# Residual loads placed behind the output weights in the queue that issues them

## The chip, the cores and the metric

The kernel runs on one core of a Trainium2 chip. The metric is the time of one execution in device microseconds (us), as the median of several runs. Besides the runs there is one profiled execution; its trace is what the prediction reads. Engines are named as the profile names them: PE (TensorE: matmuls), PEld (its weight loads), DVE (VectorE), ACT (ScalarE), POOL (GpSimd) and SP (SyncE, which here only issues DMA transfers; SPq is its queue of issues).

## The reference

One layer of an encoder on `x` (1024 tokens x 1024 columns, float32). Three sub-layers follow each other, each with a norm before it and a norm on its output, which is then added to the residual stream. The change lies at the end of the first:

```python
mix = jnp.concatenate([attn_o, dn_o], axis=-1) @ w_out[l]
x = x + _rms_norm(mix, g_mix_post[l])
c = _memory_cross_attention(_rms_norm(x, g_cross_pre[l]), _rms_norm(mem, g_mem[l]),
                            w_cq[l], w_ckv[l], w_co[l])
x = x + _rms_norm(c, g_cross_post[l])
f = _swiglu(_rms_norm(x, g_ffn_pre[l]), w_gate_up[l], w_down[l])
x = x + _rms_norm(f, g_ffn_post[l])
```

`attn_o` comes from windowed attention, `dn_o` from a gated delta rule in chunks. `w_out` is 1024 x 1024. The old `x` is the residual that is added to the normed `mix`.

## The kernel before, in words

All operands of matmuls are split into a high and a low part (`split`, L101 to L106: ACT casts to the high part at L103, DVE or POOL subtracts it from the original to get the low part at L104), and each product is the sum of three matmuls: high x high, low x high, high x low.

**Order.** The kernel is written for Tile, whose scheduler fixes the order of instructions on every engine when the program is compiled. It simulates time: at each point an engine takes, of the instructions that are ready, the one with the highest priority. Priority is the order in which the code traces them; `tc.high_priority(AHEAD)` moves what a block traces 300 places forward. `tc.issue_after(ins)` adds an edge of order alone: what the block traces on the engine of `ins` is queued behind `ins` on that engine, without a wait for its end. On the chip each queue then runs in the order so fixed, and a wait at its head holds all behind it.

**Weights.** `load_w` (L118 to L129) issues one 512 KB load of weights on SP (L125) into a tile `wraw`, and splits it into `whi` (ACT) and `wlo` (DVE or POOL). Each of the three tags has 2 buffers (`wp`, L116), so the third load waits until the first has been split. Both the load and the split are traced with high priority.

**The output projection.** Before it, L1147 loads `mix` (stored by the attention and the delta rule in `d_mix`) in two halves of 512 tokens: 4 loads of 512 KB each, into `mraw` for the first half and into a tile that the profile calls `b` for the second; each piece is split on ACT and DVE into `s0h`, `s0l` and into two `b` tiles. The last steps of the attention windows (`psw`, L685: scores; L687: mask and maximum on DVE; `ptw`, L712: transposes; `pow`, L717: values) are still under way at that time.

`mid_gemm` (L1087 to L1130) is called for the first half of the tokens (L1152) and then for the second (L1154). In each call:

- For each of 2 column halves it loads 4 pieces of `w_out` (256 rows x 512 columns, L1099), 8 in all, and runs 24 matmuls `pmg` with each (L1105). Then ACT squares the result and sums it (L1108), and DVE multiplies it with the gain into `z` (L1109).
- For each of 4 tiles of 128 tokens it loads 512 KB of residual rows, `xr`, on SP (L1115; tag `xr` has 4 buffers), gets the inverse root on POOL (L1117, L1118), and DVE adds the residual: z = z * rs + xr (L1119). `z` is stored (L1120). `xr` is then reused as the normed input of the cross-attention (L1122 to L1128).
- The second call runs `turn_norm` (L1071: transposes `ptn` on PE) on the first call's `xr` between its column halves.

The residual loads stand behind the eight weight loads in the code, but they depend on nothing else than a free buffer. After the two calls come loads of `d_mk` and `d_mv` (L1162) for the cross-attention and its query projection with weights `w_cq`.

Of the kernel before, what the change touches and what calls it, by code (L numbers as in the profile page):

```python
# [19 lines left out]
P = 128  # L20
# [56 lines left out]
def tile_hybrid_block(  # L77
# [6 lines left out]
    nc = tc.nc  # L84
# [15 lines left out]
    def split(hi, lo, src, scale=None, eng=None):  # L100

        if scale is None:
            nc.scalar.copy(hi, src)  # L103
            return (eng or nc.vector).tensor_tensor(lo, src, f32(hi), ALU.subtract)  # L104
        nc.scalar.activation(hi, src, AF.Identity, scale=scale)
        return nc.vector.scalar_tensor_tensor(lo, src, scale, f32(hi), ALU.mult, ALU.subtract)  # L106

    def pool(name, bufs, **kw):
        return tc.tile_pool(name=name, bufs=bufs, reuse_waits="tile", **kw)
# [5 lines left out]
    dram = ctx.enter_context(tc.tile_pool(name="dram", bufs=1, space=DRAM))  # L115
    wp = ctx.enter_context(pool("wp", 2))  # L116

    def load_w(src, k, n, eng=None, after=None, place=None):  # L118

        with tc.high_priority(AHEAD):  # L120
            raw = place or wp.tile([P, k, n], F32, tag="wraw", name="wraw")
            with ExitStack() as order_:
                if after:
                    order_.enter_context(tc.issue_after(after.ins))
                nc.sync.dma_start(raw, src.rearrange("(k p) n -> p k n", p=P))  # L125
            hi = wp.tile([P, k, n], F32R, tag="whi", name="whi")
            lo = wp.tile([P, k, n], F32R, tag="wlo", name="wlo")
            split(hi, lo, raw, eng=eng)
        return hi, lo  # L129
# [30 lines left out]
    def rstd_of(rs, ss, n, eps):  # L160

        w = ss.shape[-1]
        nc.gpsimd.tensor_scalar(rs, ss, n, eps, ALU.mult, ALU.add)
        nc.gpsimd.tensor_tensor(rs, rs, mhalf[:, :w], ALU.pow)
# [114 lines left out]
    def proj(src_cols, eng=None):  # L279
        whi, wlo = load_w(src_cols, KT, P, eng)  # L280
        pp = [pg.tile([P, 512], F32, tag="pg", name="pg") for _ in range(2)]
        gemm_b(whi, wlo, hT, pp)
        return pp
# [26 lines left out]
    for h in range(2):  # L310
        with tc.issue_after(ready[h][0].ins), tc.issue_after(ready[h][1].ins):
            ws.append(load_w(dcols(1, h), KT, P, after=xload[3]))
# [663 lines left out]
    def next_keys():  # L976

        ct = kv_done[0]
        kv_done[0] += 1
        whi, wlo = load_w(w_ckv[:, ct * P:(ct + 1) * P], KT, P, nc.gpsimd)  # L980
        pp = pc.tile([P, 512], F32, tag="pc", name="pck")[:, 0:ML]
        for k in range(KT):
            for i, (w, a) in enumerate(((whi, 0), (whi, 1), (wlo, 0))):
                nc.tensor.matmul(pp, w[:, k, :], mT[a][:, k, :], start=(k == 0 and i == 0), stop=(k == KT - 1 and i == 2))  # L984
        cv = mk.tile([P, 512], F32, tag="cv", name="cv", bufs=2)[:, 0:ML]
        nc.scalar.copy(cv, pp)
        nc.sync.dma_start(d_mk[ct * P:(ct + 1) * P, :], cv)
# [99 lines left out]
    def mid_gemm(tz, act, w, gp, res, dst, hf, between=None, banks=([PG] * 4, [PG] * 4), vec=False):  # L1087


        zs = [tz.tile([P, D], F32, tag="z", name="z", bufs=4) for _ in range(4)]  # L1090
        sss = [tz.tile([P, 2], F32, tag="zss", name="zss", bufs=8) for _ in range(4)]
        for ch in range(2):
            cs = slice(ch * 512, (ch + 1) * 512)
            if ch and between:
                between()

            pp = [q_.tile([P, 512], F32, tag=t_, name="pmg") for q_, t_ in banks[ch]]
            for kp in range(4):
                whi, wlo = load_w(w[kp * 256:(kp + 1) * 256, cs], 2, 512)  # L1099
                for t in range(4):  # L1100
                    tt = slice(t * P, (t + 1) * P)
                    for kk in range(2):
                        k = 2 * kp + kk
                        for i, (w_, a) in enumerate(((whi, 0), (whi, 1), (wlo, 0))):
                            nc.tensor.matmul(pp[t], act[a][:, k, tt], w_[:, kk, :], start=(k == 0 and i == 0),  # L1105
                                             stop=(k == KT - 1 and i == 2))
            for t in range(4):
                nc.scalar.activation(zs[t][:, cs], pp[t], AF.Square, accum_out=sss[t][:, ch:ch + 1])  # L1108
                nc.vector.tensor_tensor(zs[t][:, cs], pp[t], gp[:, cs], ALU.mult)  # L1109
        xn = []  # L1110
        for t in range(4):
            tok = slice(hf * HALF + t * P, hf * HALF + (t + 1) * P)
            z = zs[t]
            xr = tz.tile([P, D], F32, tag="xr", name="xr", bufs=XR)
            nc.sync.dma_start(xr, res[tok, :])  # L1115
            rs = tz.tile([P, 1], F32, tag="prs", name="prs", bufs=4)
            nc.gpsimd.tensor_scalar(rs, sss[t][:, 1:2], sss[t][:, 0:1], D * EPS, ALU.add, ALU.add)  # L1117
            nc.gpsimd.tensor_tensor(rs, rs, mhalf[:, 0:1], ALU.pow)  # L1118
            nc.vector.scalar_tensor_tensor(z, z, rs, xr, ALU.mult, ALU.add)  # L1119
            nc.sync.dma_start(dst[tok, :], z)  # L1120
            s2 = tz.tile([P, 1], F32, tag="ps2", name="ps2", bufs=4)
            nc.scalar.activation(xr, z, AF.Square, accum_out=s2)  # L1122
            r2 = tz.tile([P, 1], F32, tag="pr2", name="pr2", bufs=4)
            rstd_of(r2, s2, 1.0 / D, EPS)
            if vec:
                nc.vector.tensor_scalar(xr, z, r2, None, ALU.mult)
            else:
                nc.scalar.activation(xr, z, AF.Identity, scale=r2)  # L1128
            xn.append(xr)
        return xn  # L1130
# [12 lines left out]
    for hf in range(2):  # L1143
        for kp in range(4):
            k2 = slice(2 * kp, 2 * kp + 2)
            raw = raws[hf]
            nc.sync.dma_start(raw[:, k2, :], d_mix[kp * 256:(kp + 1) * 256, hf * HALF:(hf + 1) * HALF]  # L1147
                              .rearrange("(k p) t -> p k t", p=P))
            with tc.issue_after(marks[14].ins):
                split(mxT[hf][0][:, k2, :], mxT[hf][1][:, k2, :], raw[:, k2, :])  # L1150
    LR.close()
    xn0 = mid_gemm(tz, mxT[0], w_out, gp, x, d_x1, 0, banks=([PG] * 4, [PX] * 2 + [PN] * 2), vec=True)  # L1152
    h2T = [[opB.tile([P, KT, HALF], F32R, tag=b1, name=b1), opB_first[2]]]
    xn1 = mid_gemm(tz, mxT[1], w_out, gp, x, d_x1, 1, banks=([PG] * 4, [PX] * 2 + [PG] * 2),  # L1154
                   between=lambda: turn_norm(xn0, "cross", *h2T[0], pin=True))
    h2T.append(operand(opA, "s0"))
# [13 lines left out]
    raw = LR2.enter_context(pool("raw2", 1, side="right")).tile([P, KT, HALF], F32, name="oraw")  # L1170
# [239 lines left out]
    res = {}  # L1410
# [349 lines left out]
    def residual(t, after=None):  # L1760
        xr = tp_.tile([P, D], F32, tag="xrf", name="xrf")
        with tc.issue_after((after or late).ins):
            nc.sync.dma_start(xr, d_x2[there(t), :])
        return xr
# [62 lines left out]
    for t in range(4):  # L1827
# [19 lines left out]
        xr = residual(r)  # L1847
# [47 lines left out]
```

## Time and profile before

| | us |
|---|---|
| Median of 3 runs | 1499.31 (1497.92 to 1499.64) |
| The profiled execution | 1504.28 |
| Its span (first to last recorded work) | 1502.6 |
| PE busy in the span | 1469.4 (98%) |
| DVE busy | 1109.3 (74%) |
| ACT busy | 776.2 (52%) |

A row of the timeline gives start, duration (or, for several issues merged, the time from the first to the end of the last), engine, line, operation, out<-in and the count; in brackets stands how long the engine idled before it and what ended that. A row of a table by stretches gives from:to, its length, then busy time and count of the engines named, the granted clock of PE (1.00 is full), the busy share of the 16 DMA engines and GB/s. A row of waits names who waited for whom, the total, the number of times and the longest. All times count from the start of the span.

### The profile page before, as it was taken

How to read it: one execution, taken by the hardware profiler on the slowest of the kernel's cores; microseconds unless marked ns; L12 is line 12 of the kernel's file. 1: busy time of each engine (PE TensorE's matmuls, PEld its weight loads, DVE VectorE, ACT ScalarE, POOL GpSimd, SP SyncE). 2: the span in 40 equal slices, each digit the busy share in tenths (PEclk: the TensorE clock that was granted, in tenths of full speed). 3: DMA queues.
4: the chain of work that ended last, by engine and by line, in shares of the span. 5: the costliest groups of instructions: out<-in, count | busy, mean ns of one | idle time of the engine just before them, and what ended most of it. 6: DMA issues, size and time to landing. Idle time of an engine off the chain costs nothing.

```text
span 1502.6 us, 21339 instructions
## 1 busy us (share of the span) xinstructions
PE 1469.4 (98%) x7437; PEld 1239.6 (82%) x7437; DVE 1109.3 (74%) x1805; ACT 776.2 (52%) x1600; POOL 372.6 (25%) x410
## 2 busy tenths in 40 slices
PE   7999999999999999999999999999999999999998
PEld 6888877888889878888888877888888888888787
DVE  5878998577997866528767887676867764696666
ACT  7678844568467664555654774323223232444533
POOL 0011231442246203242201002343433342000030
PEclk9999999999999999999999999999999999999999
DMA  6244554656996585444855553443533433953355
GB/s 204 71 118 135 138 174 121 174 152 207 317 322 209 155 314 196 153 156 149 275 181 202 182 197 112 127 133 112 165 118 117 140 106 105 350 182 99 105 180 170
DMA packets 254168, 256.35 MB, mean 171 GB/s; under 512 B 18128, under 2 KB 186221, under 8 KB 254061
## 3 DMA queue, kind: packets, MB, share of 16 engines
q1 hardware_dynamic: 252141, 250.80, 52.7%
q0 software_dynamic: 768, 2.10, 0.5%
q10 hardware_dynamic: 1152, 2.10, 0.4%
q8 instruction: 58, 0.95, 0.3%
q14 instruction: 49, 0.40, 0.1%
HBM read 178.63 MB, written 73.70 MB: 168 GB/s over the span
## 4 chain that ended last, share of the span: by engine, by line
PE 68%; DVE 10%; DMA 4%; ACT 4%; issue 3%; SPq 1%; POOL 0%; DVEq 0%; ACTq 0%; POOLq 0%
PE pE L1511 7%; PE pD L1511 7%; PE pmg L1105 6%; PE pcq L276 6%; PE pdX L1733 6%; PE pA L1511 5%; PE pst L1324 5%; PE pB L1511 3%; PE pg L276 3%; PE psc L844 3%; PE pdA L1733 2%; PE pdD L1733 2%; PE pcs L1195 2%; PE pco L1222 1%; PE pck L984 1%
## 5 line engine op out<-in xcount | busy, mean ns | idle before, releaser
L103 ACT CAST whi<-wraw 128x1024 fp32r<-128x1024 f32 x96 | 100.6, 1049 | 123.3 <-DMA wraw<-in_w_gate_up_dram 39.5
L276 PE MATMUL pg<-hlo,whi 128*128 128x512 f32 x352 | 141.0, 401 | 0.0
L276 PE MATMUL pg<-hhi,whi 128*128 128x512 f32 x352 | 140.5, 399 | 0.0
L276 PE MATMUL pg<-hhi,wlo 128*128 128x512 f32 x352 | 140.2, 398 | 0.0
L104 POOL TENSOR_TENSOR wlo<-wraw,whi 128x1024 fp32r<-128x1024 f32 x36 | 88.0, 2444 | 175.8 <-ACT whi L103 163.7
L1511 PE MATMUL pA<-b,whi 128*128 128x512 f32 x352 | 109.8, 393 | 1.9 <-ACT whi L103 1.0
L104 DVE TENSOR_TENSOR wlo<-wraw,whi 128x1024 fp32r<-128x1024 f32 x60 | 74.1, 1235 | 36.1 <-ACT whi L103 31.8
L1511 PEld LDWEIGHTS pA<-b,whi 128*128 128x128 f32 x352 | 65.2, 188 | 17.1 <-ACT whi L103 1.9
L276 PEld LDWEIGHTS pg<-hhi,whi 128*128 128x128 f32 x352 | 67.3, 191 | 13.6 <-ACT hhi L241 0.3
L276 PEld LDWEIGHTS pg<-hhi,wlo 128*128 128x128 f32 x352 | 67.2, 191 | 12.6
L276 PEld LDWEIGHTS pg<-hlo,whi 128*128 128x128 f32 x352 | 67.0, 190 | 12.7
L1733 PE MATMUL pdX<-dhl,whi 128*128 128x512 f32 x264 | 76.1, 390 | 0.9 <-ACT dhl L103 0.7
L1603 POOL TENSOR_TENSOR act<-act,up 128x512 f32<-128x512 f32 x33 | 50.3, 1524 | 88.6 <-DVE up L1602 66.9
L103 ACT CAST whi<-araw 128x1024 fp32r<-128x1024 f32 (+1 forms) x36 | 35.3, 981 | 68.3 <-PE pdX L1733 27.5
L1511 PE MATMUL pA<-b,wlo 128*128 128x512 f32 x176 | 69.0, 392 | 0.5 <-DVE wlo L104 0.5
L104 DVE TENSOR_TENSOR wlo<-araw,whi 128x1024 fp32r<-128x1024 f32 (+1 forms) x36 | 40.7, 1132 | 34.2 <-ACT whi L103 34.1
L1574 POOL TENSOR_TENSOR sr<-wraw 128x512 f32<-128x512 f32 x22 | 29.9, 1357 | 139.8 <-DMA wraw<-in_w_gate_up_dram 86.4
L301 DVE SCALAR_TENSOR_TENSOR acc<-cp,cols,acc 128x1024 f32<-128x1024 f32 x48 | 63.0, 1315 | 0.2
L1733 PEld LDWEIGHTS pdX<-dhl,whi 128*128 128x128 f32 x264 | 49.3, 188 | 12.1 <-ACT dhl L103 1.1
L103 ACT CAST dhl<-b 128x512 fp32r<-128x512 f32 x66 | 40.3, 620 | 31.2 <-PE pdA L1733 13.2
L1575 DVE TENSOR_TENSOR sr<-sr,wraw 128x512 f32<-128x512 f32 x22 | 36.6, 1664 | 26.6 <-POOL sr L1574 26.6
L103 ACT CAST s0h<-sr 128x512 fp32r<-128x512 f32 x22 | 13.7, 622 | 79.3 <-POOL sr L1574 78.9
(504 smaller groups left out, 4330.2 us busy)
## 6 DMA issues: line engine op xcount, KB each, us to landing
wraw<-in_w_gate_up_dram SPq DMA_DIRECT2D x54, 512.0 KB, 3.8
kv<-d_kv SPq DMA_DIRECT2D x32, 512.0 KB, 6.2
wraw<-in_w_in_dram SPq DMA_DIRECT2D x22, 512.0 KB, 4.1
b<-in_w_down_dram SPq DMA_DIRECT2D x20, 512.0 KB, 6.5
araw<-d_as SPq DMA_DIRECT2D x20, 512.0 KB, 3.8
pz<-d_pz SPq DMA_DIRECT2D x32, 256.0 KB, 6.3
wraw<-in_w_ckv_dram SPq DMA_DIRECT2D x16, 512.0 KB, 7.1
wraw<-in_w_out_dram SPq DMA_DIRECT2D x16, 512.0 KB, 4.1
```

The lines of the kernel that those rows point to most:

```text
L103: nc.scalar.copy(hi, src)
L104: return (eng or nc.vector).tensor_tensor(lo, src, f32(hi), ALU.subtract)
L276: nc.tensor.matmul(p_, w[:, k, :], ah[a][:, k, :], start=(k == 0 and i == 0), stop=(k == nk - 1 and i == 2))
L301: nc.vector.scalar_tensor_tensor(acc, cp[:, t:t + S], taps[t], acc, ALU.mult, ALU.add)
L844: nc.tensor.matmul(out[:, d, h, :], lt[:, d, h, :], rt[:, d, h, :], start=True, stop=True)
L1105: nc.tensor.matmul(pp[t], act[a][:, k, tt], w_[:, kk, :], start=(k == 0 and i == 0), stop=(k == KT - 1 and i == 2))
L1195: nc.tensor.matmul(pp[:, t2_, :], q[a][:, ct, tt], kr_[b_][:, ct, :], start=(j == 0 and i == 0), stop=(j == 1 and i == 2))
L1324: nc.tensor.matmul(bank, a[:, tt], w, start=(start and i == 0), stop=(stop and i == 2), skip_group_check=not check)
L1511: nc.tensor.matmul(out_, w[a][:, k, :], xx[b_][:, k, :], start=(start and k == 0 and i == 0), stop=(k == HK - 1 and i == 2), skip_group_ch ...
L1575: nc.vector.tensor_tensor(s[1], s[0], a_[:, 0:HK], ALU.subtract)
L1603: nc.gpsimd.tensor_tensor(o_, o_, up, ALU.mult)
L1733: nc.tensor.matmul(banks[t], a[:, k - k0, tt], w, start=(first and k == 0 and i == 0), stop=(k == NB - 1 and i == 2), skip_group_check=not ...
```

## The change

`load_w` keeps the instruction of its latest weight load in a list. In `mid_gemm`, each residual load is traced under `issue_after` of that load, which at this place is the eighth piece of `w_out` of the same call. Both are SP instructions, so the four `xr` loads of a call are queued on SP behind the call's last weight load. There is no new instruction, tile or wait.

```diff
+    weights_in = []
+
     def load_w(src, k, n, eng=None, after=None, place=None):
...
                 if after:
                     order_.enter_context(tc.issue_after(after.ins))
-                nc.sync.dma_start(raw, src.rearrange("(k p) n -> p k n", p=P))
+                weights_in[:] = [nc.sync.dma_start(raw, src.rearrange("(k p) n -> p k n", p=P))]
...
             xr = tz.tile([P, D], F32, tag="xr", name="xr", bufs=XR)
-            nc.sync.dma_start(xr, res[tok, :])
+            with tc.issue_after(weights_in[0].ins):
+                nc.sync.dma_start(xr, res[tok, :])
```

## Prediction

> **What bounds the kernel now.** I read the page's engine line first, then the busy time of TensorE (PE) by stage, then PE's waits, then the queues around the change in order of time.
>
> ```profile
> PE 1469.4 (98%) x7437; PEld 1239.6 (82%) x7437; DVE 1109.3 (74%) x1805; ACT 776.2 (52%) x1600; POOL 372.6 (25%) x410
> ```
>
> ```profile
> 530.00:540.00 10.00, 8.04 (x33) 0.83 1.02 381
> 540.00:660.00 120.00, 120.00 (x568) 1.00 0.60 200
> 660.00:820.00 160.00, 160.00 (x829) 1.00 0.58 191
> ```
>
> The second fence is PE alone by stretches: length, busy time and (count), granted clock, DMA share, GB/s. The changed loads belong to the output projection (pmg, L1105), which begins in the first of these stretches and ends in the second. From 540 to 820 us PE is busy for 280.00 of 280 us at clock 1.00. Nothing that arrives sooner there can shorten the kernel; only something later can lengthen it. The stage has one weak place, its entrance:
>
> ```profile
> 532.00:536.00 4.00, 2.04 (x11) 1.40 (x10) 3.07 (x8) 3.88 (x6) 0.00 (x0) 0.88 1.04 396
> 536.00:540.00 4.00, 4.00 (x15) 3.30 (x15) 4.00 (x8) 3.97 (x7) 0.84 (x2) 0.70 1.05 397
> 540.00:544.00 4.00, 4.00 (x21) 3.28 (x20) 3.66 (x9) 3.27 (x10) 0.00 (x0) 1.00 1.03 405
> ```
>
> Here all engines are listed (PE, PEld, DVE, ACT, POOL), then clock, DMA share, GB/s. PE idles 4.00 - 2.04 = 1.96 us, and the clock falls short by 0.12 x 4 + 0.30 x 4 = 1.7 us. So the entrance loses 3.7 us. DMA is saturated at about 400 GB/s, and the moved loads are part of that load, so the question is whether they cause the loss.
>
> ```profile
> 526.13 0.41 SPq L125 DMA_DIRECT2D wraw<-in_w_out_dram  x1
> 530.99 2.14 SPq L1115 DMA_DIRECT2D xr<-in_x_dram  x3
> 534.20 0.38 SPq L125 DMA_DIRECT2D wraw<-in_w_out_dram  x1
> 535.51 0.33 SPq L1115 DMA_DIRECT2D xr<-in_x_dram  x1
> 539.61 0.38 SPq L125 DMA_DIRECT2D wraw<-in_w_out_dram  x1
> ```
>
> ```profile
> 534.42 0.39 PE L685 MATMUL psw<-khi,qs 128*128 128x256 f32 x1 [1.92 <-DVE m L687]
> ```
>
> ```profile
> 531.66 1.05 ACT L103 CAST whi<-wraw 128x1024 fp32r<-128x1024 f32 x1 [5.33 <-DMA wraw<-in_w_out_dram]
> 532.74 1.23 DVE L104 TENSOR_TENSOR wlo<-wraw,whi 128x1024 fp32r<-128x1024 f32 x1 [4.82 <-ACT whi L103]
> 533.88 0.48 DVE L687 CUSTOM_DVE_ANT_0 sc<-psw,C,prm 128x256 f32<-128x256 f32 x1
> ```
>
> Call the first half's eight pieces of the output weights p0 to p7, the second half's q0 to q7. PE's idle piece ends at 534.42 with a score matmul (psw, L685) that waits for L687 on VectorE. That stands behind p0's low part, this behind p0's cast, and this behind p0's landing at 531.66. p0 was issued at 526.13, the first residual load (xr) at 530.99, 4.9 us later and behind it in the same queue. The moved loads come after the cause, so **the 3.7 us are not theirs.**
>
> **The change part by part.**
>
> *Removed at 531.* Four issues leave the SP queue (2.14 + 0.33 = 2.5 us of issue time) and 4 x 512 KB = 2.1 MB leave the DMA queue, 2.1 MB / 405 GB/s = 5.2 us of it. p2 (534.20) still waits for its buffer: p0's low part ends at 532.74 + 1.23 = 533.97. It lands up to 1.5 MB / 0.4 = about 4 us sooner. What does SP itself save?
>
> ```profile
> SPq L125 <- DMA mraw<-d_mix: 2.0, 2, 1.0
> SPq L1162 <- DMA xr<-in_x_dram: 0.8, 1, 0.8
> ```
>
> These are SP's waits for earlier transfers (total, times, longest); so p3 and the memory-value load go at most about 1 us sooner. On the path to the end this is worth 0.0 us: p2's and p3's matmuls already run without a gap (540 to 820 us, above). The bounds are 0 and the entrance's 3.7 us, since that is all PE loses here; I take 0, because p0 precedes xr in the queue.
>
> *Added behind p7.* Since issue_after sets order and no wait, xr goes out as soon as p7 has been issued.
>
> ```profile
> 559.86 0.37 SPq L1147 DMA_DIRECT2D b<-d_mix  x1
> 565.70 0.37 SPq L125 DMA_DIRECT2D wraw<-in_w_out_dram  x1
> 566.23 1.39 SPq L1147 DMA_DIRECT2D b<-d_mix  x3
> 571.08 11.25 SPq L125 DMA_DIRECT2D wraw<-in_w_out_dram  x3
> ```
>
> ```profile
> 584.13 1.27 DVE L1119 SCALAR_TENSOR_TENSOR z<-z,prs,xr 128x1024 f32<-128x1024 f32 x1
> ```
>
> ```profile
> L1071 PE MATMUL ptn<-ident,xr x64: 270/272/274, 606.9 to 670.5; 128*128 128x128 f32 x64
> ```
>
> p7 goes at 565.70, q0 at 571.08. The first reader of xr, L1119, runs at 584.13, 18 us after p7. Four issues take 2.5 us and 2.1 MB take 5.2 us, so xr is there by about 580 us even behind the three activation loads (b). L1119 therefore loses nothing, and its results are not transposed on PE until 606.9.
>
> What is queued behind the moved loads? If they go **behind b**, only q0. It is issued at 571.08 and would land 5.2 us later.
>
> ```profile
> 576.00:580.00 4.00, 4.00 (x19) 3.31 (x18) 2.36 (x2) 1.33 (x3) 0.00 (x0) 1.00 0.11 15
> ```
>
> ```profile
> 579.63 1.05 ACT L103 CAST whi<-wraw 128x1024 fp32r<-128x1024 f32 x1 [2.67 <-PE pmg L1105]
> 585.10 1.07 PE L1105 MATMUL pmg<-whi,b 128*128 128x512 f32 x4
> ```
>
> The DMA queue is all but empty from 576 to 580 (15 GB/s), so q0 has landed by 576 now and by about 581.2 then. Its cast now runs at 579.63, held by PE and not by DMA; at 581.2 it would end by 582.3, and PE wants q0 at 585.10. Cost 0, with 2.8 us to spare; the DMA gap is the cover.
>
> If they go **ahead of b**, all three b loads land up to 5.2 us later, and this is where the schedule is thin:
>
> ```profile
> 572.29 1.05 ACT L103 CAST b<-b 128x1024 fp32r<-128x1024 f32 x1 [2.49 <-DMA b<-d_mix]
> 573.65 1.06 ACT L103 CAST b<-b 128x1024 fp32r<-128x1024 f32 x1 [0.30 <-DMA b<-d_mix]
> 574.96 1.06 ACT L103 CAST b<-b 128x1024 fp32r<-128x1024 f32 x1 [0.26 <-DMA b<-d_mix]
> 575.91 1.05 ACT L103 CAST whi<-wraw 128x1024 fp32r<-128x1024 f32 x1
> 577.19 1.22 DVE L104 TENSOR_TENSOR wlo<-wraw,whi 128x1024 fp32r<-128x1024 f32 x1
> 579.66 0.39 PE L1105 MATMUL pmg<-whi,s0h 128*128 128x512 f32 x1
> 580.79 0.39 PE L1105 MATMUL pmg<-wlo,s0h 128*128 128x512 f32 x1
> ```
>
> ScalarE (ACT) casts three b pieces, each held by its DMA, and then p7 (575.91). p7's high part is ready at 576.96 and PE wants it at 579.66: 2.7 us of slack. The low part is ready at 578.41 and wanted at 580.79: 2.4 us. A delay of 5.2 us with the same ACT order stalls PE by 5.2 - 2.4 = 2.8 us. With p7 ahead of b in ACT's order it costs nothing: b itself is wanted at 585.10 and has until then.
>
> Which order is it? After the first b load (559.86) SP stood free until 565.70 without taking the other three, so the compiler's order did not count them ready before p7; xr counts as ready at once. I lean to some of xr ahead of b. But ACT's order is made by the same scheduling pass, which then sees b late and p7's buffer free at about 574.2 (p7's 24 matmuls run from 579.66 to 585.10, 5.44 us, so p6's began 5.44 us ahead of them and p5's were over), and can put p7 first. The bounds of this edit are 0 and the stall; I take 0, the nearer to rows in which every piece has over 2 us of slack.
>
> *The second half.* Its four loads already stand behind q7, the last output-weight load:
>
> ```profile
> 603.73 5.80 SPq L125 DMA_DIRECT2D wraw<-in_w_out_dram  x2
> 628.19 1.29 SPq L1115 DMA_DIRECT2D xr<-in_x_dram  x3
> 630.00 0.85 SPq L1115 DMA_DIRECT2D xr<-in_x_dram  x1
> ```
>
> So here the new edge changes nothing: 0.
>
> *The order drawn anew.* The compiler orders all engines' queues by a simulated time; a different SP order can swap neighbours anywhere later. No row shows this. For bounds I use PE's waits:
>
> ```profile
> PE pA L1511 <- ACT whi L103: 1.0, 2, 0.8
> PE pA L1511 <- ACT m L1531: 0.9, 2, 0.7
> ```
>
> These two are the largest after 660 us; the stage's own is the 1.92 us before L685. A swap can win or cost about as much as one of these, -1.9 to +1.9 us; I take 0.
>
> *What a stall adds.* The entrance shows that an idle stretch of 2 us is followed by a half clock: the windows above give 1.7 us lost. A stall of 2.8 us at p7 would then cost 2.8 + 1.7 = 4.5 us. The Trainium skill, "TensorE: Matmul & The Clock Gate", Part 1 (the table of the two states), says that the clock drops after an idle window of about 3.4 us. By that rule the same stall would cost 2.8 us alone, and the slow rival below would come out at 1502.1 us instead, which moves its chance to no change. The trace disagrees with it: 1.96 us of idle time in 532 to 536 sufficed. I go by the trace.
>
> **The sum.** 0 (removed) + 0 (added) + 0 (second half) + 0 (order) = 0. The profiled execution took 1504.28 us, 1.68 beyond its span of 1502.6 and 4.97 above the median of the runs. A difference of 0 is 1504.28 for it and 1499.31 for the median, so I forecast **1499.3 us**.
>
> **The rivals.**
>
> *A, no change in the time (forecast).* For it speaks PE's full row from 540 to 820 us. With the order's bounds it is 1497.4 to 1501.2.
>
> *B, slower: b behind xr.* xr goes ahead of the three b loads, the ACT order stays, and p7's cast waits. It decides from a delay of 2.4 us on, which is two of the four loads (1.3 us each). Full price 4.5 us: 1503.8. For it: xr is ready at once, b was not. Against it: ACT's order is drawn by the same pass.
>
> *C, faster: the entrance closes.* With less ahead of it the compiler draws the order around 532 us anew, so that L687 no longer stands behind p0's low part; the idle time and the half clock go: -3.7 us, 1495.6. For it: DMA at 397 GB/s there. Against it: p0 was issued 4.9 us before the first xr.
>
> *D, slower elsewhere.* The new order breaks a tight place after 632 us, with a stall and a half clock as at the entrance: +3.7 us, 1503.0. For it: PE's two waits after 660 us of about 1 us show places without slack. Against it: each is small, and the SP order after 603 us is the same.
>
> That the change does not do what it says holds for half of it, the second half's loads, and is contained in A.
>
> **How the numbers follow.** About 0.2%, 3.0 us, is what a measurement of this kernel can tell from no change; so "same" is 1496.3 to 1502.3. I give A 0.50, B 0.24, C 0.16 and D 0.10. B's partial delays, under 3 us, would count as same; I leave its whole chance on the slow side, since D's price is as uncertain in the other direction. Faster 0.16, same 0.50, slower 0.34. The range reaches down over most of C (1496.0; its far end, 1495.6, is left out) and up over B (1504.0). A's own range, 1497.4 to 1501.2, stands beside it.
>
> **What would show it.** Right: in the changed profile PE is busy for all of 540 to 660, the xr issues stand behind p7 near 566 us, the idle time before L685 near 532 is still about 1.9 us with a half clock after it, and p7's cast starts before about 578. B is right if ACT shows a b cast held by DMA until about 580 with p7's cast behind it and PE idle before a pmg matmul. C is right if 532 to 540 shows PE busy at clock 1.00. D is right if 530 to 632 is unchanged and a new wait stands in PE's list later. The forecast is wrong if PE idles anywhere in 540 to 660, or if the order near 526, before any moved load, has changed.

## The result and the profile after

The changed kernel is **slower**: median 1504.68 us (1501.02 to 1509.37, 21 runs) against 1499.85 us for the kernel before, measured beside it (1497.92 to 1508.08, 21 runs). The ratio is 1.0024 with a 95% interval of 1.0015 to 1.0033, that is 2.2 to 5.0 us of 1500 (the quotient of the two medians, 1.0032, lies at its upper end). The forecast was no change, 1499.3 us; the median lies 0.7 us above the range given.

The two profiled executions hide this. Both spans are 1502.6 us, and the engine line of the page is the same to 1.4 us:

```profile
PE 1468.4 (98%) x7437; PEld 1238.2 (82%) x7437; DVE 1108.7 (74%) x1805; ACT 776.2 (52%) x1600; POOL 372.3 (25%) x410
```

So the stage has to be read by itself. PE alone by stretches, after (the columns are those of the same view of before):

```profile
530.00:540.00 10.00, 8.75 (x41) 1.00 1.03 389
540.00:660.00 120.00, 116.83 (x545) 0.99 0.56 191
660.00:820.00 160.00, 160.00 (x828) 1.00 0.57 191
```

Two things have moved. The stretch of the entrance (530 to 540) is busier than before and at full clock; this execution ran ahead of the other (below), and part of its idle time lies ahead of 530. And the 120 us that were full before have a hole of 120.00 - 116.83 = 3.17 us. The waits of PE between 500 and 660 us say whose it is; before had only the first half's `psw` wait of 1.9 us here:

```profile
PE pmg L1107 <- ACT whi L103: 3.2, 1, 3.2
PE psw L687 <- DVE m L689: 1.6, 1, 1.6
PE ptw L714 <- DVE m L689: 0.2, 1, 0.2
```

The entrance's idle time is nearly what it was (1.6 + 0.2 against 1.9 us). The new wait is a matmul of the output projection (L1107 now, L1105 before) that waits for ACT's cast of a weight piece. In the timeline of PE it is one row, the first matmul of p7:

```profile
578.58 0.50 PE L1107 MATMUL pmg<-whi,s0h 128*128 128x512 f32 x1 [3.17 <-ACT whi L103]
```

All engines by stretches around it (PE, PEld, DVE, ACT, POOL, then the granted clock, DMA share, GB/s):

```profile
576.00:580.00 4.00, 1.42 (x5) 1.15 (x6) 3.61 (x4) 3.65 (x5) 0.00 (x0) 0.90 0.26 97
580.00:584.00 4.00, 4.00 (x14) 3.16 (x13) 2.31 (x3) 1.25 (x3) 0.00 (x0) 0.67 0.48 152
```

The clock falls short by 0.10 x 4 + 0.33 x 4 = 1.7 us after the hole. So p7 costs 3.17 + 1.7 = 4.9 us in this execution. What ACT did meanwhile:

```profile
572.97 1.05 ACT L103 CAST b<-b 128x1024 fp32r<-128x1024 f32 x1 [7.57 <-DMA b<-d_mix]
575.18 1.04 ACT L103 CAST b<-b 128x1024 fp32r<-128x1024 f32 x1 [1.16 <-DMA b<-d_mix]
576.53 1.04 ACT L103 CAST b<-b 128x1024 fp32r<-128x1024 f32 x1 [0.31 <-DMA b<-d_mix]
577.49 1.04 ACT L103 CAST whi<-wraw 128x1024 fp32r<-128x1024 f32 x1
578.43 1.05 ACT L103 CAST b<-b 128x1024 fp32r<-128x1024 f32 x1
```

ACT stood idle for 7.57 us at the head of its queue for a b piece, cast three of them, and only then p7 (577.49), whose load is the last of the four in the first row of SP and was issued by 561.39 (542.97 + 18.42), 16 us earlier:

```profile
542.97 18.42 SPq L127 DMA_DIRECT2D wraw<-in_w_out_dram  x4
561.44 2.10 SPq L1118 DMA_DIRECT2D xr<-in_x_dram  x4
563.71 6.38 SPq L1150 DMA_DIRECT2D b<-d_mix  x4
570.20 12.45 SPq L127 DMA_DIRECT2D wraw<-in_w_out_dram  x3
```

The moved loads stand behind p7 and ahead of all four b loads. Before, the first b load had gone out ahead of p7 and the other three right behind it. SP has a new wait, too, for the last window's store of `d_mix`, of which b reads a part:

```profile
SPq L1150 <- DMA d_mix<-ao: 4.3, 1, 4.3
```

The page's list of DMA issues, asked for 556 to 572 us, gives the time from issue to landing of that store (last column), in before and then after:

```profile
d_mix<-ao POOLq DMA_DIRECT2D x1, 128.0 KB, 2.4
```

```profile
d_mix<-ao POOLq DMA_DIRECT2D x1, 128.0 KB, 6.1
```

**Why the profiled pair is equal.** The compiled orders of the two kernels differ only between about 531 and 600 us, and yet after's execution issued p0 2.7 us earlier (526.13 before):

```profile
523.43 0.41 SPq L127 DMA_DIRECT2D wraw<-in_w_out_dram  x1
```

This is a difference of executions, ahead of anything moved. Adding up what after's execution gained: 2.7 us of that, and at the entrance 0.2 us less idle time and no half clock (1.7 us), make 4.6 us, against 4.9 us lost at p7. One execution of each would have shown nothing.

**What the compiler redrew.** Read instruction by instruction from the two traces, POOL's order is the same. On SP, besides the xr loads, the loads of `mkr` and `mvr` stand together ahead of p4, and p7 stands ahead of all b loads. On ACT and DVE, the casts and subtractions for `kr` and `vr` come earlier, the end of the last attention window (`ao`, which is then stored) later, and ACT's order is p6, b, b, b, p7, b where it was b, p6, b, b, b, p7.

### The profile page after: what moved, and what is told of

It is laid out like the page before. It is cut to its first block, busy times and chain, and to the rows that moved or that the text cites. A ratio compares the mean times of both kernels' runs of the same rounds, so it can differ in the third digit from the quotient of the medians.

```text
span 1502.6 us, 21344 instructions
## 1 busy us (share of the span) xinstructions
PE 1468.4 (98%) x7437; PEld 1238.2 (82%) x7437; DVE 1108.7 (74%) x1805; ACT 776.2 (52%) x1600; POOL 372.3 (25%) x410
## 4 chain that ended last, share of the span: by engine, by line
PE 77%; DVE 9%; issue 5%; DMA 5%; ACT 2%; SPq 1%; POOL 0%; DVEq 0%; ACTq 0%; POOLq 0%
PE pg L278 11%; PE pE L1514 8%; PE pD L1514 8%; PE pA L1514 6%; PE pcq L278 6%; PE pdX L1736 6%; PE pst L1327 5%; PE pdA L1736 4%; PE pB L1514 4%; PE pmg L1107 3%; PE psc L846 2%; PE pdD L1736 2%; PE pcs L1198 2%; PE pco L1225 1%; DMA rr<-rr 1%
```

## The experiments

The first theory was the prediction's rival B: xr stands ahead of b in the DMA queue, b is late, and p7's cast stands behind b's casts (the queue theory). Its rival: the removal from 531 us redraws the order of the whole stage, and what costs is that order, with or without xr ahead of b (the removal theory). In all texts "removal" and "addition" mean the first half's four loads; q0 is the second half's first weight piece. Each kernel was compared with the kernel before on the same chip.

### e1: xr also behind b

```diff
-            with tc.issue_after(weights_in[0].ins):
+            with tc.issue_after(weights_in[0].ins), tc.issue_after(mix_in[0].ins):
                 nc.sync.dma_start(xr, res[tok, :])
...
+            mix_in[:] = [nc.sync.dma_start(raw[:, k2, :], d_mix[...])]
```

> The four residual loads of the first half stay behind p7 and are queued behind the four b loads as well (SP: p7, b x4, xr x4). Queue theory (p7's cast stands on ScalarE behind b casts that wait for loads which the residual loads hold up): b lands about 5.2 us sooner than in the changed kernel, p7's cast ends before PE wants it, PE's 3.2 us wait at pmg and the half clock behind it go; PE busy for all of 540 to 660 but for 0.3 us; ratio to before 0.999 to 1.001. Load theory (2.1 MB moved into this stretch cost, in whatever order): the stall stays within 1 us of 3.2 us, ratio about 1.002. Order theory (the redrawn order between 540 and 560 costs, not the stall): the order there is the changed kernel's, so the ratio stays about 1.002 even if the stall goes.

Measured: 1.0045 (1.0027 to 1.0063). PE's wait, then SP and ACT in order of time:

```profile
PE pmg L1107 <- ACT whi L103: 3.8, 1, 3.8
```

```profile
564.77 8.29 SPq L1151 DMA_DIRECT2D b<-d_mix  x4
573.10 1.90 SPq L1118 DMA_DIRECT2D xr<-in_x_dram  x4
```

```profile
570.20 1.05 ACT L103 CAST b<-b 128x1024 fp32r<-128x1024 f32 x1 [6.06 <-DMA b<-d_mix]
574.90 1.04 ACT L103 CAST b<-b 128x1024 fp32r<-128x1024 f32 x1 [3.66 <-DMA b<-d_mix]
575.86 1.04 ACT L103 CAST whi<-wraw 128x1024 fp32r<-128x1024 f32 x1
```

xr stands behind b, and the stall is still there: ACT waits for b twice and casts a weight piece (p6 now) behind that. SP's four b issues take 8.29 us, 5.3 of them a wait for the `d_mix` store. So xr ahead of b is not needed for a stall: the queue theory does not hold as the whole cause. It is not empty either. From the first b issue to ACT's first two casts of b it is 5.4 and 10.1 us here (564.77 to 570.20 and 574.90), and 9.3 and 11.5 us in after (563.71 to 572.97 and 575.18), where xr stands ahead. ACT's order is another one than after's, too: here p6 stands behind two b, there p7 behind three.

### e2: casts of b behind p7's

After's loads; the splits of the second half's b pieces are queued behind p7's on ACT and DVE.

```diff
+    for kp in range(4):
+        k2 = slice(2 * kp, 2 * kp + 2)
+        with tc.issue_after(last_cast.ins), tc.issue_after(last_cut.ins):
+            split(mxT[1][0][:, k2, :], mxT[1][1][:, k2, :], raws[1][:, k2, :])
```

> SP's order is that of the changed kernel (p7, xr x4, b x4); only the casts and low parts of the four b pieces are queued behind p7's on ScalarE and VectorE. Queue theory: p7's cast runs as soon as p5's buffer is free, PE's wait at pmg falls from 3.2 us to under 0.3 us, b is split by 582 and PE wants it at about 582, so at most 1 us is lost there; ratio 0.999 to 1.001. Load theory: b lands as late as before and the loss stays, ratio about 1.002, with the wait at the first matmul that reads b. Order theory: ratio about 1.002.

Measured: 1.0026 (1.0009 to 1.0043).

```profile
PE pmg L1109 <- DVE wlo L106: 2.0, 1, 2.0
```

The wait for p6 or p7 is gone, and a smaller one stands further on. In the timeline of PE it is a matmul with the low part of q2, the second half's third weight piece:

```profile
598.35 0.50 PE L1109 MATMUL pmg<-wlo,b 128*128 128x512 f32 x1 [1.95 <-DVE wlo L106]
```

On DVE that low part stands behind the residual adds of the first half, these stand behind q0's low part, and q0's cast comes behind the last b cast:

```profile
580.46 1.05 ACT L105 CAST b<-b 128x1024 fp32r<-128x1024 f32 x1 [0.28 <-DMA b<-d_mix]
582.12 1.05 ACT L105 CAST whi<-wraw 128x1024 fp32r<-128x1024 f32 x1 [0.60 <-PE pmg L1109]
```

The profile names PE as what ended the last 0.60 us, but p6's matmuls, which held the buffer, had ended near 577.6; q0's own load, behind xr and b in the queue, is the likelier one. In e10 (below), which has the same casts and no xr, p7's cast starts at the same 572.10, q0's at 578.05, 4.1 us sooner, and q2's low part 4.0 us sooner. With xr ahead of b, b and q0 are too late for this order too.

### e3: half of xr ahead of b

```diff
-            with tc.issue_after(weights_in[0].ins):
+            with tc.issue_after((weights_in if t < 2 else mix_in)[0].ins):
```

> Two residual loads stand ahead of the b loads, two behind them (SP: p7, xr x2, b x4, xr x2); on ScalarE p7's cast stands behind all four b casts, where it was behind three. Queue theory: b's last piece lands 2.6 us sooner than in the changed kernel, at about 575.2 in its time, p7's cast ends near 577.2 where PE wants it at 575.3: a wait of about 2 us (1 to 2.5), with a half clock of up to 1.7 us behind it if the idle stretch covers enough of the clock's window; ratio 1.001 to 1.002. Load theory: the same amount of data in the same stretch, so the whole 3.2 us stay. Order theory: ratio 1.002.

Measured: 1.0030 (1.0016 to 1.0044).

```profile
PE pmg L1107 <- ACT whi L103: 3.1, 1, 3.1
```

```profile
572.80 1.05 ACT L103 CAST b<-b 128x1024 fp32r<-128x1024 f32 x1 [0.54 <-DMA b<-d_mix]
575.57 1.04 ACT L103 CAST b<-b 128x1024 fp32r<-128x1024 f32 x1 [1.72 <-DMA b<-d_mix]
```

Half of the bytes ahead of b, and the same stall, but not the same order: ACT now casts four b pieces, then p7. The third b cast starts 12.3 us after the first xr issue (560.55 to 572.80), against 15.1 us in after (561.44 to 576.53), so fewer bytes ahead do bring b sooner; the fourth cast, which stood behind p7 in after, takes that back. This run cannot tell the amount from the order.

### e4: the removal alone

The kernel before; the first half's xr is filled with zeros on GpSimd and not loaded (this leaves the first half's residual out of the output).

```diff
-            nc.sync.dma_start(xr, res[tok, :])
+            if hf == 0:
+                nc.gpsimd.memset(xr, 0.0)
+            else:
+                nc.sync.dma_start(xr, res[tok, :])
```

> The kernel before, but the first half's four residual tiles are set to zero on GpSimd and not loaded: the removal alone, with nothing put behind p7 (the first half's residual is left out of the sum). Removal theory (without these loads near 531 the compiler draws the order from 540 to 565 anew: p7 is issued ahead of the first b load, the last window's store comes later, and b's casts stand on ScalarE ahead of p6 and p7): PE waits 3 to 4.5 us at pmg for a cast, as where b stands ahead of the residual loads; ratio 1.002 to 1.006. Queue theory of the prediction (the residual loads ahead of b are the cause): nothing holds b up, no wait at pmg, ratio 0.998 to 1.001.

Measured: 1.0050 (1.0032 to 1.0069). PE's wait, SP and ACT:

```profile
PE pmg L1105 <- ACT whi L103: 4.0, 1, 4.0
```

```profile
560.04 8.51 SPq L1150 DMA_DIRECT2D b<-d_mix  x4
```

```profile
565.60 1.05 ACT L103 CAST b<-b 128x1024 fp32r<-128x1024 f32 x1 [6.20 <-DMA b<-d_mix]
570.36 1.04 ACT L103 CAST b<-b 128x1024 fp32r<-128x1024 f32 x1 [3.71 <-DMA b<-d_mix]
571.31 1.04 ACT L103 CAST whi<-wraw 128x1024 fp32r<-128x1024 f32 x1
```

Two megabytes less to move, nothing put in their place, and the kernel is 0.5% slower. The picture is e1's, with two b ahead of p6 on ACT; ACT, DVE and PE have the same order in both, so the zeros that GpSimd writes here (near 515 us) are not the cause. **The removal alone is enough to cost.**

### e5: twice the bytes behind p7

After, with a copy of the same rows to a scratch tensor behind each xr load.

```diff
+            if hf == 0:
+                with tc.issue_after(weights_in[0].ins):
+                    nc.sync.dma_start(d_more[tok, :], res[tok, :])
```

> Behind each of the first half's four residual loads the same rows are also copied into a scratch buffer that nobody reads: twice the data ahead of the b loads. The compiler, which now sees b later still, puts p7's cast ahead of the four b casts by itself. Queue theory: no wait at p7 (under 0.3 us) although DMA carries 2.1 MB more; b lands near 580 to 583 and the second half's first matmuls may wait for it by up to 1.5 us; ratio 0.999 to 1.002, not above the changed kernel's. Load theory: twice the data, about twice the stall, 6 us or more, ratio 1.004 or above. Order theory: ratio about 1.002.

Measured: 1.0056 (1.0038 to 1.0074).

```profile
PE pmg L1108 <- ACT whi L103: 5.1, 1, 5.1
```

The place was not the one of after: with b that late the compiler itself put p6 and p7 ahead of b on ACT, no wait stands at p7, and the 5.1 us stand at the second half's first matmul. So xr ahead of b has a price as well; the order decides where it is paid.

### e6: the addition alone

After, with four dummy loads of the same size where xr stood (into `z`, which is overwritten later). The compiled order of ACT, DVE and POOL is then before's, with xr behind p7 and all b loads on SP.

```diff
+            if hf == 0 and ch == 0:
+                for t in range(4):
+                    nc.sync.dma_start(zs[t], res[t * P:(t + 1) * P, :])
```

> The changed kernel with four loads of the same size put where the residual loads stood near 531, into the tiles z that are overwritten later: the addition alone (residual loads behind p7) on the order of the kernel before (SP: b, p7, b x3, xr x4; ScalarE as before). Removal theory: no wait at pmg, PE busy for all of 540 to 660, ratio 0.999 to 1.001, though DMA carries 2.1 MB more. Queue theory: here the residual loads stand behind b, so it expects the same; a wait at the second half's first weights of up to 1 us would show a price of the addition. Load theory: ratio 1.002 or more.

Measured: 1.0013 (1.0000 to 1.0026). PE by stretches, and ACT's cast of q0:

```profile
560.00:600.00 40.00, 40.00 (x178) 1.00 0.71 252
```

```profile
580.46 1.05 ACT L103 CAST whi<-wraw 128x1024 fp32r<-128x1024 f32 x1 [4.84 <-DMA wraw<-in_w_out_dram]
```

PE is full, there is no `pmg` wait, and q0, now behind xr, lands at 580.46 us, 0.7 us from the 581.2 worked out in the prediction. The `d_mix` store lands in 2.4 us, as in before. With the removal's place filled the order stays, and the moved loads, behind b, cost at most 0.26% (0.999 to 1.001 was expected).

### e8: the b piece that needs the store last

The pieces of b in the order 0, 2, 3, 1; the last window's store goes into piece 1.

```diff
-        for kp in range(4):
+        for kp in ((0, 1, 2, 3), (0, 2, 3, 1))[hf]:
```

> The changed kernel with the second half's four pieces of mix in the order 0, 2, 3, 1: the piece with the last window's rows comes last, so that only it waits on SP for that window's store. If that wait holds up b: the three casts ahead of p7's end about 1 to 1.5 us sooner and PE's wait at pmg falls from 3.2 to 1.5 to 2.3 us; ratio 1.001 to 1.002. If the residual loads ahead of b are all of the delay: the wait stays at 3 us, ratio 1.002.

Measured: 1.0018 (1.0005 to 1.0030). PE's wait and SP's:

```profile
PE pmg L1107 <- ACT whi L103: 2.1, 1, 2.1
```

```profile
SPq L1150 <- DMA d_mix<-ao: 2.9, 1, 2.9
```

SP's wait falls by 1.4 us (4.3 in after), PE's by 1.0 us (3.17 to 2.15). The late store is part of the stall. The other 2.1 us stay, although none of the three b casts ahead of p7 needs the store any more: those loads are issued behind p7 and stand behind xr.

### e9: e1 and e2 together

> The changed kernel with the residual loads behind the b loads, and the casts and low parts of b behind p7's on ScalarE and VectorE. The b loads still wait on SP for the last window's store (about 5 us). Removal theory with the head of the line on ScalarE as its last step: p6 and p7 are cast when their buffers come free, b is split by about 580, before PE wants it near 584, so no wait at pmg above 0.3 us; ratio 0.999 to 1.001. If the lateness of b itself is the price, the wait moves to the second half's first matmul, 1 us or more, ratio 1.001 to 1.003.

Its diff is those of e1 and e2. Measured: 1.0026 (1.0013 to 1.0040). PE's waits and ACT's row of q0:

```profile
PE pmg L1109 <- ACT whi L105: 2.7, 1, 2.7
PE pmg L1109 <- DVE wlo L106: 1.9, 1, 1.9
```

```profile
577.85 1.04 ACT L105 CAST whi<-wraw 128x1024 fp32r<-128x1024 f32 x1 [6.51 <-DMA wraw<-in_w_out_dram]
```

No wait at p6 or p7; b is in time. But q0 now stands behind b and xr and lands at 577.85. PE waits 2.7 us for it, and 1.9 us more for q2's low part, by e2's way. The pair moves the wait and does not end it.

### e10: e4's loads with e2's casts

> The loads of e4_none (the first half's residual loads taken away and xr filled with zeros on GpSimd, so the first half's residual is left out of the output), with the casts of the four b pieces queued behind the eighth weight piece's on ACT and DVE. Removal theory with the ACT order as its last step: the redrawn SP order and the late store remain, so SP still waits over 3 us for d_mix before b, but no wait of PE for p6 or p7 over 0.3 us is left, PE is full from 540 to 580, and the ratio comes down from 1.005 to 0.999 to 1.002. If the wait only moves on, it shows at the second half's first matmul, 1 to 3 us, ratio 1.002 to 1.004. Rival (the removal costs somewhere else, the casts only mark the place): the ratio stays at 1.004 or above with PE idle as long as before in sum.

Its diff is those of e4 and e2. Measured: 1.0016 (1.0002 to 1.0031). SP's wait and PE by stretches:

```profile
SPq L1154 <- DMA d_mix<-ao: 5.3, 1, 5.3
```

```profile
560.00:600.00 40.00, 40.00 (x178) 1.00 0.61 211
```

The loads, the late store and SP's wait are those of e4. Only the casts and low parts of b stand behind p7's, and the 4.0 us of stall are gone. So the last link is the order of ACT and DVE, where DVE's low part of a piece follows ACT's cast.

### e11: the suspected order in the kernel before

The kernel before; only p6 and p7's splits are queued behind the casts of all four b pieces. The loads are untouched.

```diff
+                if behind_b:
+                    order_.enter_context(tc.issue_after(behind_b[0].ins))
                 split(hi, lo, raw, eng=eng)
...
+                behind_b[:] = [b_cast] * (hf == 0 and ch == 1 and kp >= 2)
                 whi, wlo = load_w(w[kp * 256:(kp + 1) * 256, cs], 2, 512)
```

> The kernel before with one thing set by hand: the casts and splits of p6 and p7 stand behind the casts of all four b pieces on ACT and DVE. The loads of xr stay where they were. Theory (a weight cast behind b casts that are held by DMA): the last b cast ends near 576 us, p6 is cast near 577 and is wanted near 574, so PE idles 2 to 4 us before a matmul of p6 or p7, plus up to 1.7 us of half clock; ratio 1.002 to 1.004. Rival (the cost comes from the changed queue order on SP, not from ACT's): PE idles less than 1 us there and the ratio is 0.999 to 1.001.

Measured: 1.0035 (1.0024 to 1.0047).

```profile
PE pmg L1114 <- ACT whi L105: 2.4, 1, 2.4
```

```profile
569.86 1.05 ACT L105 CAST b<-b 128x1024 fp32r<-128x1024 f32 x1 [6.14 <-DMA b<-d_mix]
572.50 1.05 ACT L105 CAST b<-b 128x1024 fp32r<-128x1024 f32 x1 [0.25 <-DMA b<-d_mix]
573.45 1.99 ACT L105 CAST whi<-wraw 128x1024 fp32r<-128x1024 f32 x2
```

The residual loads are where they always were, and the stall is there with its mark: weight casts behind b casts that wait for their DMAs. An order of that kind, put in by hand (b four times, then p6 and p7; after has p6, three b, p7), makes the kernel slower by about as much as the change does. (The half clock that could have followed did not come: 1.00 from 560 to 600.)

### e12: another small load moved

The kernel before; the broadcast load of the norm's gain and its scaling are queued behind the first half's activation loads and the first of their casts.

```diff
+    with tc.issue_after(first_in[-1].ins), tc.issue_after(first_cast[0].ins):
+        nc.sync.dma_start(gp, g_mix_post[0].partition_broadcast(P))
+        nc.scalar.mul(gp, gp, math.sqrt(D))
```

> The kernel before with another small load moved: the broadcast load of the output norm's gain and its scaling are queued behind the four loads of the first half's activations and the first of their casts. xr stays where it was. In its compiled order all four b loads stand behind p7 and ACT casts b, b, b, p6, b, p7. Theory (what costs is that ACT order, whatever moved): PE idles 2 to 4 us before a matmul of p6, SP waits over 2 us for d_mix, ratio 1.002 to 1.005. Rival (the cost needs the residual loads to have moved): no wait over 0.5 us before pmg, ratio 0.998 to 1.001.

Measured: 1.0053 (1.0039 to 1.0068). PE's waits:

```profile
PE pmg L1107 <- ACT whi L105: 6.0, 1, 6.0
PE pmg L1107 <- DVE ao L723: 0.5, 1, 0.5
```

A move that has nothing to do with the residual gives the same kind of stall at the same place, larger than foreseen (6.0 us; 2 to 4 were expected).

### e13: xr behind q0, casts of b behind p7's

The version that the runs pointed to as the best. ACT, DVE and PE have the order of e10, and SP has it with xr behind q0, which is traced earlier for that.

```diff
+        if hf == 0:
+            last_cast[:] = [casts_[0], cuts[0]]
+            ahead.append(load_w(w[:256, :512], 2, 512))
```

> The changed kernel with the first half's residual loads one place further back, behind the second half's first weight load, which is traced ahead of them for that, and with the casts of b behind the eighth weight piece's. ACT, DVE and PE then have the same order as in e10_none_casts, and SP has it with the four residual loads behind the second half's first weight load. Theory (what is left of the cost in e2_cast_first and e9_both is the residual loads standing ahead of that weight load or of b, and nothing else): no wait before pmg over 0.3 us, PE full from 560 to 660, ratio 0.999 to 1.002. Rival (the new order costs also without a wait of PE in this stage): PE full there, and the ratio at 1.003 or more.

Measured: 1.0008 (0.9996 to 1.0020).

```profile
PE pmg L1109 <- DVE wlo L106: 1.0, 1, 1.0
```

A wait of 1.0 us is left, for q2's low part as in e2, against at most 0.3 expected: q1 stands behind xr now, and its cast waits 3.75 us for its load. The kernel cannot be told from the kernel before, and it does not beat it.

### The runs together

PE's waits before `pmg` (us) and the clock lost from 560 to 600 us (1 minus the granted clock, times 40), from each kernel's profiled execution, beside the ratio:

| kernel | PE waits | clock | sum | ratio |
|---|---|---|---|---|
| before | 0 | 0 | 0 | 1 |
| after | 3.2 | 1.6 | 4.8 | 1.0024 |
| e1 xr behind b | 3.8 | 3.6 | 7.4 | 1.0045 |
| e2 casts behind p7 | 2.0 | 0 | 2.0 | 1.0026 |
| e3 half | 3.1 | 1.6 | 4.7 | 1.0030 |
| e4 removal alone | 4.0 | 1.6 | 5.6 | 1.0050 |
| e5 twice the bytes | 5.1 | 1.6 | 6.7 | 1.0056 |
| e6 addition alone | 0 | 0 | 0 | 1.0013 |
| e8 piece 1 last | 2.1 | 1.6 | 3.7 | 1.0018 |
| e9 e1 and e2 | 4.6 | 1.6 | 6.2 | 1.0026 |
| e10 e4 and e2 | 0 | 0 | 0 | 1.0016 |
| e11 order by hand | 2.4 | 0 | 2.4 | 1.0035 |
| e12 gain late | 6.5 | 3.6 | 10.1 | 1.0053 |
| e13 behind q0 | 1.0 | 0 | 1.0 | 1.0008 |

Every kernel with 2 us or more of wait is slower, and those without one lie within 0.16%. Sums and ratios agree only to 2 or 3 us (an interval of a ratio is about 2 us to each side, and each sum is from one execution). Six kernels lose 1.7 to 2.9 us more than this stage shows (e2, e4, e5, e6, e10, e11), e9 and e12 some 2 us less, the other five agree within 1.2 us. The entrance, where the clock lost from 530 to 540 us was 0 to 3.4 us in these executions, is not in the table. e2, e9, e10 and e13 have one order on ACT, DVE and PE and differ only in xr's place on SP: ahead of b, behind b, not there, behind q0. Their waits of 2.0, 4.6, 0 and 1.0 us are the price of the addition in that order. Where e6 and e10 lose their 0.13 and 0.16% was not found; their intervals begin at 1.0000 and 1.0002.

## Why the prediction was wrong, point by point

- **What bounds the kernel: right.** PE was full from 540 to 820 us, and the loss came as something later in just that stretch.
- **Removed at 531, 0 taken: the step that failed.** The prediction priced only what would arrive sooner, with bounds of 0 and a gain, and saw that nothing could be won. It did not ask what order the compiler draws without these loads. e4 shows the removal alone at +0.5%, with 4.0 us of stall.
- **The order drawn anew, -1.9 to +1.9 us and 0 taken: too small, and read at the wrong place.** The bound was taken from PE's waits after 660 us and from the entrance; what the new order put on PE lay at p7, 4.9 us. The rows that would have told were in the prediction: p7's slack of 2.4 us, with three b casts ahead of it that wait for DMAs. (The store by POOL that b waits for stands in no row of it.) Here the new order has its price where slack is thin and a queue mixes late and early work: 4.0 us in e4, and none in e10, where that place is pinned.
- **Added behind p7: right in one order, wrong in the other.** With before's order, xr behind b costs q0 what was worked out (e6, above). The lean to xr ahead of b was right as well. That the same pass could then put p7 first on ACT, for which it took 0, was wrong for the changed kernel: it put p6 first, and p7 behind three b. In e5 it did put p7 first.
- **The second half, 0: right.** Its SP order is the same.
- **What a stall adds, 1.7 us: right here, and not a rule.** 1.7 us were measured after 3.17 us. That an idle stretch of 2 us brings it was read from one stretch: after 2.0 us in e2 and 2.4 us in e11 the clock stayed at 1.00. The Trainium skill, "TensorE: Matmul & The Clock Gate", Part 1, has the clock drop after an idle window of about 3.4 us; the trace after shows it after 3.17 us, as the one before did after 1.96 us.
- **Rival B: right in place, instruction and size** (2.8 + 1.7 = 4.5 us foreseen, 3.17 + 1.7 = 4.9 measured, 1503.8 against 1504.68 us), **only a part in its cause, so the near hit in size is in part luck.** xr ahead of b does delay b in the changed kernel (e1's and e3's rows). But it is not what the stall needs: e1, with xr behind b, and e4, without xr, have one too. There b is late because all of it is issued behind p7 and its second piece waits for the `d_mix` store, which lands 4.8 to 6.4 us after its issue in all kernels whose b loads stand behind p7, xr or not, and 2.4 us in before, e6 and e11. In after the store accounts for 1.0 of the 3.17 us (e8).
- **Rival C: wrong.** The idle time at the entrance stayed (1.6 + 0.2 us). The half clock was missing in after's execution, but in the ten kernels whose xr left 531 it was there in five.
- **Rival D: wrong.** PE's waits after 660 us are the same but for one of 0.3 us.
- **The signs.** One was blunt: p7's cast was to start "before about 578", and it started at 577.49, with PE idle. After's execution ran 4.25 us ahead there (p7's first matmul was due at 578.58 - 3.17 = 575.41, and came at 579.66 before). A time in the span is a sign only against what wants the result.

What stays open. That the compiler redraws this stretch is seen in the compiled orders; why just these swaps follow from four loads less was not traced through its simulation. That the store lands late because b or xr loads are issued just ahead of it is argued from the landing times; a kernel that changes that alone was not run.

## What to carry to other kernels

In a kernel whose engine orders a scheduler fixes, taking a load away is an edit of the order too: list the places near it where an engine's queue holds work that is waited for behind work that waits for a DMA, and price each at its stall, in both directions. Where the slack is thin there (2.4 us here), pin that order by hand before loads are moved (in e10, 4 us of stall went away by that alone), and look where the late piece shows up next (e2, e9, e13). And do not compare two single executions for 0.3%: the pair here had equal spans.

## What the runs showed of the hardware

- A 128 KB store of POOL's software queue landed in 2.4 us where SP's latest 512 KB load had been issued 3.8 us ahead of it (before, e6, e11), and in 4.8 to 6.4 us where one had been issued at most 0.9 us ahead (the other eleven).
- PE's clock after an idle stretch is not a matter of its length alone: it fell after 2.1 us (e8, 0.96 from 560 to 600 us), and stayed at 1.00 after 2.0 us (e2) and 2.4 us (e11). After stretches of 3.1 to 6.0 us it fell each time (six of six: after, e1, e3, e4, e5, e12), by 1.6 to 3.6 us of work.
